# A hybrid decoder layer on one core: queries turned on VectorE ahead of their store instead of on TensorE after their load, and the norm vectors in one laid-out load

## The chip, the cores and the metric

The kernel runs on one core of a Trainium2 chip. The core has four engines that compute, each with its own instruction stream in program order: TensorE (PE: matrix products and transposes, which write to PSUM; its weight loads are shown apart as PEld), VectorE (DVE), ScalarE (ACT) and GpSimd (POOL). SyncE (SP) computes nothing and issues most of the DMAs; POOL and ACT issue a few. The metric is the device time of one execution in microseconds, as the median of several runs. The time before is 1201.64 us, the median of three (1200.92 to 1206.23).

## The reference

One layer (DEPTH 1) over x of 1024 tokens by 1024 channels, all in float32. A norm and one projection give queries, three pairs of keys and values, gates and the inputs of a short convolution. Attention runs over compressed, selected and windowed keys; its output and the convolution's go through an output projection, and a squared-ReLU MLP follows. Cut to what matters here:

```python
h = rms_norm(x, g_mix_norm[l])
z = h @ w_in[l]
q, kc, vc, ks_, vs_, kw_, vw_, gl, hc, cg, bg = jnp.split(z, offs, axis=-1)
q = rms_norm(q.reshape(B, T, N_ATTN_HEADS, HEAD_DIM), g_q[l])      # 8 heads of 64
k_cmp = rms_norm(compress(kc, pe, w1, b1, w2, b2), g_k[l, 0])
k_slc = rms_norm(ks_.reshape(kv_shape), g_k[l, 1])                 # 2 groups of 64
k_win = rms_norm(kw_.reshape(kv_shape), g_k[l, 2])
gates = jax.nn.sigmoid(gl)
attn_out = nsa_attention(q, k_cmp, v_cmp, k_slc, v_slc, k_win, v_win, gates)
conv_out = short_conv_mixer(hc, cg, bg, conv_w[l])
x = x + concat(rms_norm(attn_out, ...), rms_norm(conv_out, ...)) @ w_o[l]
h = rms_norm(x, g_ffn_norm[l])
x = x + jnp.square(jax.nn.relu(h @ w_up[l])) @ w_down[l]
```

Scores are products of a query with keys over the 64 channels of a head, so on TensorE both must stand with channels on the partitions.

## The kernel before

The 1024 tokens are eight blocks (tb) of 128. Numbers are split into a high part of reduced precision and the remainder, and a product is made of three matmuls (high by high, high by low, low by high) with 512 columns each; `copy_act` on ScalarE writes the high part, a subtraction on VectorE or POOL the low part.

**Order.** The code calls a planner (class `Plan`) in place of the engines. It records every instruction with what it depends on, gives each a modelled cost (`Plan.cost`), lays out the whole kernel in a model of the engines, and shakes the due times with the seeds in the tuple `SEEDS`, one after the other, to arrive at the order in which the instructions are then issued on each engine. `plan.follow` makes an instruction wait in that plan for others, and `plan.slack` lets the planner expect a DMA to land later than modelled by that many us. So an edit anywhere can move instructions everywhere. All recorded instructions bear the same line in the profile, L272, and are told apart by their tiles.

**Start.** The loads of x, of its transpose and of weights are issued on SP. `norm_in` (L751) loads an x block `xt`, sums its squares and keeps the load in the list `last`; `x_in` loads and splits parts of the transpose; `token_sums` adds and subtracts token halves (tiles x, t1, t2, t4) on VectorE, with high parts on ScalarE. At L786 to L790 the norm vectors g_q and g_k are loaded by POOL, each copied to all 128 partitions by the DMA, after the sixth `xt` load (`last[5]`) in the plan; VectorE then multiplies `gk_bc` by `gq_bc`. So g_q is applied to the keys, not to the queries. TensorE runs the first projection into PSUM tiles `zp` of a pool of five; ScalarE empties them to `z`, and `k_norm` (L834) scales the keys with `gk_bc`.

**Compression.** `compress_steps` (from L876) makes the compressed keys and values in small steps between the query blocks. Its biases `b1_bc` and `b2_bc`, for keys and values together, are loaded at L869 to L874 by POOL.

**Query projection.** For each of the eight blocks (loop at L964) ScalarE empties `zp` to `z`, the eight heads are normed, and `qn` is filled: per head 128 numbers, 64 of the high part and 64 of the low part, with the high part first for the heads of group 0 and second for those of group 1. The row of 1024 numbers of each token goes to the DRAM tile `q_d` in one DMA of 512 KB on SP. `qn` has one buffer.

**Attention.** `queries(tb)` (L1305) brings one block back. For each of two groups g it loads 256 KB of `q_d` into `qx` (one buffer), turns the four heads with one TensorE transpose each into a PSUM tile `tpq` of the pool `psP` (three buffers, tag pt, shared with the transposes of probabilities `tp`), and ScalarE copies `tpq` to `Qg` (three buffers). POOL then copies half of `Qg` to `Qz` (two buffers). `scores(tb, g, ...)` multiplies `Qg` and `Qz` with the keys; VectorE adds distances and takes the maxima (`nm`), ScalarE the exponentials (`pt`), POOL weighs them; `weigh` turns the probabilities (`tp`), splits them (`ph` on ScalarE, `pl` on VectorE) and multiplies with the values (`ot`); `finish` applies the output projection (`wa`). The blocks are taken in the order 3, 2, 1, 0, 4, 5, 7, 6; a block's queries are fetched while the block before it is worked on. The output projection of the convolution (`wc`) is mixed with the first block. The MLP follows, from about 570 us to the end.

Of the kernel before, what the change touches and what calls it, by code (L numbers as in the profile page):

```python
# [10 lines left out]
F32 = mybir.dt.float32  # L11
F32R = mybir.dt.float32r
# [136 lines left out]
        self.seen, self.nodes, self.tile = [], [], None  # L149


SEEDS = (1000006, 1000008, 1000012, 1000028, 1000030, 1000044, 1000056, 1000071, 1000072, 1000073, 1000097, 1000113, 1000123, 1000168, 1000170, 1000178, 1000184, 1000230, 1000235, 1000280, 1000295, 1000299, 1000300, 1000339, 1000349, 1000363, 1000373, 1000406, 1000407, 1000433, 1000445, 1000463, 1000475, 1000479, 1000518, 1000523, 1000551, 1000553, 1000556, 1000560, 1000561, 1000602, 1000631, 1000682, 1000684, 1000744, 1000762, 1000820, 1000883, 1000891, 1000903, 1000927, 1000943, 1000964, 1000972, 1001010, 1001014, 1001117, 1001141, 1001179, 1001212, 1001309, 1001376, 1001383, 1001417, 1001453, 1001528, 1001689, 1001701, 1001732, 1001749, 1001991, 1002049, 1002060, 1002190, 1002305, 1002330, 1002338, 1002354, 1002415, 1002550, 1002569, 1002695, 1002710, 1002984, 1002988, 1003029, 1003125, 1003214, 1003231, 1003262, 1003316, 1003351, 1003576, 1003644, 1003759, 1003795, 1004123, 1004570, 1004698, 1004784, 1004785, 1004924, 1005022, 1005212, 1005620, 1006475, 1006959, 1007873, 1008004, 1008352, 1008594, 1008648, 1008693, 1008873, 1008934, 1009028, 1009032, 1009107, 1009286, 1009381, 1009543, 1009791, 1009963, 1010063, 1010079, 1010468, 1010509, 1010514, 1010529, 1011124, 1011195, 1011915, 1011946, 1012041, 1012076, 1012380, 1012411, 1012893, 1013770, 1013959, 1014076, 1014304, 1014500, 1014729, 1014772, 1014939, 1015200, 1015293, 1016011, 1016217, 1016447, 1016524, 1016643, 1016685, 1017381, 1018464, 1019062, 1019171, 1019208, 1019743, 1019760, 1019965, 1020196, 1020244, 1020564, 1020709, 1022567, 1022787, 1023841, 1024288, 1025052, 1025417, 1026259, 1028122, 1028301, 1028583, 1029752, 1031086, 1031370, 1032572, 1032854, 1033263, 1033296, 1033397, 1033540, 1033583, 1033891, 1034930, 1036525,)


class Plan:
# [146 lines left out]
    def cost(self, name, method, a, kw, views):  # L302
# [23 lines left out]
        if name == "DVE":  # L326
            self.port = near and n > 1 and (method in ("tensor_tensor", "scalar_tensor_tensor", "tensor_copy")
                                            or method == "tensor_scalar" and n != 12)
            if method == "tensor_tensor_reduce":
                self.port = False  # L330
                c = .079 + n * .00104 + .06 * isinstance(kw.get("scalar"), View)
                return c, c + .13, 0
            if method == "scalar_tensor_tensor":
                c = .1 + n * .0011 if n >= 200 else .11 + n * .0012
            elif method == "tensor_scalar":
                c = .06 + n * .00059 + (.05 if n < 64 else 0)
            elif method == "memset":
# [262 lines left out]


@with_exitstack
def trunk_layer(ctx, tc, x, x_t, vectors, w_in, g_q, g_k, w_cmp1, b_cmp1, w_cmp2, b_cmp2,
                w_o, w_up, w_down, out):
# [4 lines left out]
    w_in, g_q, g_k = w_in[0], g_q[0], g_k[0]  # L609
# [12 lines left out]
    def tt(eng, o, a, b, op):  # L622
        eng.tensor_tensor(o, a, b, op=op)
# [63 lines left out]
    hTl = [(twp, htp)[i].tile([P, KD, 512], F32R, name=f"hTl{i}") for i in range(2)]  # L687

    kcn = twp.tile([P, 2 * HD], F32, name="kcn")
    gq_bc = twp.tile([P, HD], F32, name="gq_bc")  # L690
    gk_bc = twp.tile([P, 3, HD], F32, name="gk_bc")
    TD = {n: [htp.tile([P, 4, 512], F32R, name=f"{n}{q}") for q in "hl"] for n in ("t1", "t2")}
    wp = pool(wp_stack, "wp", bufs=4, side="right")
    psP_stack = ctx.enter_context(ExitStack())
# [88 lines left out]
        x_in(k, 1)  # L783
    for tb in range(4, NT):
        norm_in(tb)
    plan.follow = (last[5],)  # L786
    nc.gpsimd.dma_start(gq_bc, g_q.partition_broadcast(P))
    nc.gpsimd.dma_start(gk_bc, g_k.partition_broadcast(P))
    plan.follow = ()
    tt(nc.vector, gk_bc, gk_bc, gq_bc.unsqueeze(1).to_broadcast([P, 3, HD]), ALU.mult)  # L790

# [41 lines left out]
    with b1:  # L833
# [32 lines left out]
        xp_stack.close()  # L866
        cs = b1.enter_context(ExitStack())
        cp = pool(cs, "cp", side="right")
        b1_bc = cp.tile([P, 2, 256], F32, name="b1_bc")  # L869
        b2_bc = cp.tile([P, 2, HD], F32, name="b2_bc")  # L870
        plan.follow = (last[-1],)
        nc.gpsimd.dma_start(b1_bc, b_cmp1.partition_broadcast(P))
        nc.gpsimd.dma_start(b2_bc, b_cmp2.partition_broadcast(P))
        plan.follow = ()  # L874

        def compress_steps():  # L876
            for kv in range(2):
                yield
                ch = cp.tile([P, 16, HD], F32, name="ch")
                for g in range(G):  # L880
                    plan.slack = 3.5
# [39 lines left out]
                tt(nc.vector, hx, hp[:, :256], b1_bc[:, kv], ALU.add)  # L921
# [16 lines left out]
                if kv == 0:  # L938
# [4 lines left out]
                    tt(nc.vector, kc, cps[:, :HD], b2_bc[:, 0], ALU.add)  # L943
                    sq = cp.tile([P, HD], F32, name="kcsq")
                    ss = st.tile([P, 1], F32, name="ss")
                    nc.scalar.activation(sq, kc, AF.Square, accum_out=ss)
                    ri = st.tile([P, 1], F32, name="ri")
# [3 lines left out]
                else:  # L951
                    for g in range(G):
                        cps = psB.tile([P, 512], F32, name="cps", tag="mm")
                        for j in range(2):
                            nc.tensor.matmul(cps[:64, :HD], hT[:, j, g * 64:(g + 1) * 64], w2[:, j],
                                             start=j == 0, stop=j == 1)
                        vc = cp.tile([64, HD], F32, name="vcr")
                        tt(nc.vector, vc, cps[:64, :HD], b2_bc[:64, 1], ALU.add)
# [5 lines left out]
        for tb, ps in (a for tbs in (QUADS[1], (0,), (1,), (2,), (3,)) for a in z_tokens(pieces, tbs, 512, steps, 1)):  # L964
# [19 lines left out]

        plan.plus = 12
        for _ in steps:
# [22 lines left out]
    with ExitStack() as b2:  # L1009
# [809 lines left out]
    plan.issue()  # L1819


_INS = ['x', 'x_t', 'vectors', 'w_in', 'g_q', 'g_k', 'w_cmp1', 'b_cmp1', 'w_cmp2', 'b_cmp2', 'w_o', 'w_up', 'w_down']
# [32 lines left out]
```

## Time and profile before

| | us |
|---|---|
| median of three runs | 1201.64 |
| profiled execution | 1202.77 |
| its span, first to last instruction | 1201.0 |
| DVE busy in the span | 909.1 |
| ACT busy in the span | 698.4 |
| POOL busy in the span | 726.4 |

The profile shows one execution. A busy TensorE in it counts a matmul from its start to its modelled end; matmuls overlap, so what one costs the stream is read from the distance between starts. "A <- B" in brackets behind an instruction means that its engine stood idle before it and what released it. Times in the timeline are from the start of the span.

The transfers that the change deals with stand thus in the list of DMAs (KB each, and median us from issue to landing): q_d<-qn 8 of 512 KB, 4.2 us; qx<-q_d 16 of 256 KB, 2.7 us.

### The profile page before, as it was taken

The numbers are of one execution on the slowest core, as the hardware profiler recorded it, in microseconds if no ns is written. First come the engines' busy times: TensorE is split into PE (matmuls) and PEld (weight loads), VectorE is DVE, ScalarE is ACT, GpSimd is POOL, SyncE is SP. The second block draws the span as 40 slices with busy tenths as digits, with TensorE's granted clock in tenths as the row PEclk, the third lists the DMA queues.
The fourth block names the chain that finished last, engine by engine and source line by source line (L and its number), as shares of the span: only waits on it lengthen the run. The fifth ranks groups of instructions, "written<-read, shape, count | busy, mean of one in ns | idle before, by whom it ended". The sixth has DMA issues, their size and how long they took to land.

```text
span 1201.0 us, 18151 instructions
## 1 busy us (share of the span) xinstructions
PE 1189.2 (99%) x5893; PEld 991.4 (83%) x5893; DVE 909.1 (76%) x1800; ACT 698.4 (58%) x1551; POOL 726.4 (60%) x663
## 2 busy tenths in 40 slices
PE   9999999999999999999999999999999999999998
PEld 7788988888888888888788888888888888888887
DVE  7748868785798989998875665554468988888885
ACT  7678634352599878888855545555345434434440
POOL 1544400020376553534978878787889899888971
PEclk9999999999999999999999999999999999999999
DMA  9765531256112110003155354443559445543513
GB/s 337 184 166 180 167 79 36 71 175 211 46 52 71 36 36 19 27 19 109 50 167 176 121 186 141 149 158 132 184 192 399 145 149 177 168 163 112 163 44 140
DMA packets 106702, 160.24 MB, mean 133 GB/s; under 512 B 20592, under 2 KB 58752, under 8 KB 106608
## 3 DMA queue, kind: packets, MB, share of 16 engines
q1 hardware_dynamic: 100320, 151.25, 38.5%
q10 hardware_dynamic: 5520, 5.28, 1.3%
q0 software_dynamic: 768, 2.56, 0.8%
q8 instruction: 46, 0.75, 0.3%
q14 instruction: 48, 0.39, 0.1%
HBM read 110.82 MB, written 48.23 MB: 132 GB/s over the span
## 4 chain that ended last, share of the span: by engine, by line
PE 88%; DVE 5%; DMA 2%; ACT 2%; issue 1%; SPq 0%; POOL 0%; DVEq 0%; ACTq 0%
PE X L272 28%; PE Z L272 18%; PE tp L272 6%; PE zX L272 5%; PE zp L272 5%; PE ot L272 5%; PE wa L272 4%; PE wc L272 3%; PE W L272 3%; PE zZ L272 3%; PE zW L272 1%; PE hp L272 1%; DMA qx<-q_d 1%; DVE hTl L272 1%; DVE pl L272 1%
## 5 line engine op out<-in xcount | busy, mean ns | idle before, releaser
L272 PE MATMUL X<-we,uu 128*128 128x512 f32 x720 | 196.1, 389 | 0.1
L272 PE MATMUL Z<-we,uu 128*128 128x512 f32 (+1 forms) x582 | 163.5, 387 | 0.5 <-DVE y L272 0.5
L272 PEld LDWEIGHTS X<-we,uu 128*128 128x128 f32 x720 | 135.1, 188 | 28.6 <-DVE y L272 0.6
L272 ACT ACTIVATE uu<-ur 128x512 fp32r<-128x512 f32 x108 | 66.9, 631 | 131.6 <-PE Z L272 71.5
L272 PEld LDWEIGHTS Z<-we,uu 128*128 128x128 f32 x582 | 108.6, 188 | 23.0 <-DVE y L272 0.7
L272 ACT ACTIVATE pt<-pt,nm 128x640 f32<-128x640 f32 (+7 forms) x128 | 93.8, 735 | 26.8 <-DVE nm L272 26.5
L272 POOL TENSOR_TENSOR d<-d 128x512 f32<-128x512 f32 x64 | 98.7, 1558 | 10.0 <-DVE d L272 8.4
L272 DVE TENSOR_TENSOR pl<-tp,ph 128x512 fp32r<-128x512 f32 (+1 forms) x148 | 94.8, 654 | 6.5 <-ACT ph L272 5.3
L272 DVE TENSOR_TENSOR y<-X,y 128x512 f32<-128x512 f32 x128 | 84.2, 681 | 13.4 <-PE X L272 13.2
L272 PE MATMUL tp<-ident,pt 128*128 128x128 f32 x528 | 93.6, 273 | 0.4 <-DVE nm L272 0.4
L272 ACT ACTIVATE ph<-tp 128x512 fp32r<-128x512 f32 (+1 forms) x148 | 81.5, 571 | 17.5 <-PE tp L272 12.2
L272 DVE TENSOR_TENSOR y<-Z,y 128x512 f32<-128x512 f32 (+1 forms) x97 | 65.2, 681 | 31.6 <-PE Z L272 30.8
L272 POOL TENSOR_TENSOR uu<-ur,uu 128x512 fp32r<-128x512 f32 x54 | 83.4, 1547 | 3.2 <-ACT uu L272 3.1
L272 ACT ACTIVATE we<-s 128x512 fp32r<-128x512 f32 x55 | 34.6, 630 | 82.6 <-PE X L272 35.1
L272 PEld LDWEIGHTS tp<-ident,pt 128*128 128x128 f32 x528 | 67.2, 141 | 12.2 <-issue 0.8
L272 POOL MEMSET Qz<- 64x512 f32 x16 | 8.3, 520 | 111.1 <-PE zX L272 104.8
L272 PE MATMUL zp<-w_hi,hTh 128*128 128x512 f32 (+1 forms) x192 | 66.1, 369 | 3.2 <-ACT z L272 2.7
L272 PE MATMUL zp<-w_lo,hTh 128*128 128x512 f32 (+1 forms) x192 | 66.8, 364 | 0.0
L272 PE MATMUL zp<-w_hi,hTl 128*128 128x512 f32 (+1 forms) x192 | 65.4, 364 | 0.0
L272 POOL TENSOR_TENSOR we<-wd,we 128x512 fp32r<-128x512 f32 x32 | 46.9, 1467 | 29.1 <-ACT we L272 29.0
L272 POOL TENSOR_TENSOR pt<-pt,rr 128x640 f32<-128x640 f32 (+4 forms) x64 | 62.2, 1001 | 0.0
L272 ACT ACTIVATE we<-wu 128x512 fp32r<-128x512 f32 x57 | 35.9, 630 | 44.6 <-PE X L272 30.0
(1340 smaller groups left out, 3649.1 us busy)
## 6 DMA issues: line engine op xcount, KB each, us to landing
u_d<-d SPq DMA_DIRECT2D x112, 256.0 KB, 2.7
ur<-u_d SPq DMA_DIRECT2D x108, 256.0 KB, 2.9
wu<-in_w_up_dram SPq DMA_DIRECT2D x16, 1024.0 KB, 6.0
wd<-in_w_down_dram SPq DMA_DIRECT2D x16, 1024.0 KB, 6.9
xt<-in_x_dram SPq DMA_DIRECT2D x10, 512.0 KB, 7.1
x<-in_x_t_dram SPq DMA_DIRECT2D x16, 256.0 KB, 6.7
w1r<-in_w_cmp_dram SPq DMA_DIRECT2D x16, 256.0 KB, 2.8
q_d<-qn SPq DMA_DIRECT2D x8, 512.0 KB, 4.2
```

Source lines behind the costliest of these rows:

```text
L272: node.do.append(lambda: getattr(engine, method)(*[real(x) for x in a], **{k: real(x) for k, x in kw.items()}))
```

## The change

The queries are turned before they are stored. After `z` is scaled, VectorE transposes it in blocks of 32 by 32 into a new tile `zT` (one buffer): within each such block, channels stand on the partitions and tokens along the row. ScalarE and VectorE write the high and low parts of `zT` to `qn`, whose row is now ordered by group, by quarter c (two of the high part and two of the low part, each 32 channels), by head and by 32 tokens. The store to `q_d` keeps its size and its one DMA.

`queries` loads each group in four DMAs of 64 KB on SP, one for each quarter: it puts the four 32-partition blocks of a quarter side by side in 32 partitions of `qx`. So `qx` holds 128 channels on the partitions, and ScalarE copies it to `Qg` with its dimensions swapped. The transposes on TensorE and the PSUM tile `tpq` are gone.

The norm vectors come from the host as one array `g_qk` of 128 rows (the same 256 numbers on each) and are loaded by SP in one DMA, after the second `xt` load in the plan, with a slack of 3 us. The biases of the compression are loaded for keys and values apart, the second pair into the same buffer. Squares of the compressed keys go to a tile that exists already. The planner gets a price for VectorE's transpose, and a new tuple of seeds (203 in place of 190).

```diff
+            if method == "transpose":
+                self.port = True
+                return .07 + n * .00104, .15 + n * .00104, 0
...
-    gq_bc = twp.tile([P, HD], F32, name="gq_bc")
-    gk_bc = twp.tile([P, 3, HD], F32, name="gk_bc")
+    g_bc = twp.tile([P, 4, HD], F32, name="g_bc")
+    gq_bc, gk_bc = g_bc[:, 0], g_bc[:, 1:]
...
-    plan.follow = (last[5],)
-    nc.gpsimd.dma_start(gq_bc, g_q.partition_broadcast(P))
-    nc.gpsimd.dma_start(gk_bc, g_k.partition_broadcast(P))
+    plan.follow = (last[1],)
+    plan.slack = 3.0
+    nc.sync.dma_start(g_bc, g_qk.rearrange("p (n d) -> p n d", d=HD))
+    plan.slack = 0.0
     plan.follow = ()
     tt(nc.vector, gk_bc, gk_bc, gq_bc.unsqueeze(1).to_broadcast([P, 3, HD]), ALU.mult)
...
-        b1_bc = cp.tile([P, 2, 256], F32, name="b1_bc")
-        b2_bc = cp.tile([P, 2, HD], F32, name="b2_bc")
-        plan.follow = (last[-1],)
-        nc.gpsimd.dma_start(b1_bc, b_cmp1.partition_broadcast(P))
-        nc.gpsimd.dma_start(b2_bc, b_cmp2.partition_broadcast(P))
-        plan.follow = ()
...
             for kv in range(2):
                 yield
+                b1_bc = cp.tile([P, 256], F32, name="b1_bc")
+                b2_bc = cp.tile([P, HD], F32, name="b2_bc")
+                plan.follow = () if kv else (last[-1],)
+                nc.gpsimd.dma_start(b1_bc, b_cmp1[kv].partition_broadcast(P))
+                nc.gpsimd.dma_start(b2_bc, b_cmp2[kv].partition_broadcast(P))
+                plan.follow = ()
...
-                    sq = cp.tile([P, HD], F32, name="kcsq")
+                    sq = zt.tile([P, HD], BF16, name="ksq", bufs=2)
...
-            qn = zt.tile([P, H, 2, HD], F32R, name="qn", bufs=1)
+            qn = zt.tile([P, G, 4, R, 32], F32R, name="qn", bufs=1)
             zh = z.rearrange("p (h d) -> p h d", h=H)
             tt(nc.vector, zh, zh, ri.unsqueeze(2).to_broadcast([P, H, HD]), ALU.mult)
+            zT = zt.tile([P, 512], F32, name="zT", bufs=1)
+            nc.vector.transpose(zT, z)
             for g in range(G):
-                zg = z[:, g * 256:(g + 1) * 256].rearrange("p (r d) -> p r d", r=R)
-                qg = qn[:, g * R:(g + 1) * R]
-                copy_act(qg[:, :, g], zg)
-                tt(nc.vector, qg[:, :, 1 - g], zg, qg[:, :, g].bitcast(F32), ALU.subtract)
-            nc.sync.dma_start(q_d[tb * P:(tb + 1) * P], qn.rearrange("p h a d -> p (h a d)").bitcast(F32))
+                zg = zT[:, g * 256:(g + 1) * 256].rearrange("p (r c t) -> p c r t", r=R, c=2)
+                hi, lo = qn[:, g, 2 * g:2 * g + 2], qn[:, g, 2 - 2 * g:4 - 2 * g]
+                copy_act(hi, zg)
+                tt(nc.vector, lo, zg, hi.bitcast(F32), ALU.subtract)
+            nc.sync.dma_start(q_d[tb * P:(tb + 1) * P], qn.rearrange("p g c r t -> p (g c r t)").bitcast(F32))
...
-                qx = kp.tile([P, R, 2, HD], F32, name="qx", bufs=1)
-                q_load.append(nc.sync.dma_start(qx.rearrange("p h a d -> p (h a d)"),
-                                                q_d[tb * P:(tb + 1) * P, g * 512:(g + 1) * 512]))
-                tp = psP.tile([P, 4, P], F32, name="tpq", tag="pt")
-                for r in range(R):
-                    nc.tensor.transpose(tp[:, r], qx[:, r].rearrange("p a d -> p (a d)"), ident)
+                qx = kp.tile([P, 4, R, 32], F32, name="qx", bufs=1)
+                for c in range(4):
+                    q_load.append(nc.sync.dma_start(
+                        qx[c * 32:(c + 1) * 32].rearrange("p b r t -> p b (r t)"),
+                        q_d[tb * P:(tb + 1) * P, (4 * g + c) * P:(4 * g + c + 1) * P].rearrange("(b p) n -> p b n", b=4)))
                 Qg = kp.tile([P, R, P], F32R, name="Qg", bufs=3)
                 Qz = kp.tile([P, R, P], F32R, name="Qz", bufs=2)
-                copy_act(Qg, tp)
+                copy_act(Qg.rearrange("p r (b t) -> p b r t", b=4), qx)
...
+    a["g_qk"] = np.tile(np.concatenate([a[n].reshape(-1) for n in ("g_q", "g_k")]), (P, 1))
```

More of the change, by code (lines that the diff above doesn't have):

```diff
@@ L149, in __init__ @@
         self.seen, self.nodes, self.tile = [], [], None
-SEEDS = (1000006, 1000008, 1000012, 1000028, 1000030, 1000044, 1000056, 1000071, 1000072, 1000073, 1000097, 1000113, 1000123, 1000168, 1000170, 1000178, 1000184, 1000230, 1000235, 1000280, 1000295, 1000299, 1000300, 1000339, 1000349, 1000363, 1000373, 1000406, 1000407, 1000433, 1000445, 1000463, 1000475, 1000479, 1000518, 1000523, 1000551, 1000553, 1000556, 1000560, 1000561, 1000602, 1000631, 1000682, 1000684, 1000744, 1000762, 1000820, 1000883, 1000891, 1000903, 1000927, 1000943, 1000964, 1000972, 1001010, 1001014, 1001117, 1001141, 1001179, 1001212, 1001309, 1001376, 1001383, 1001417, 1001453, 1001528, 1001689, 1001701, 1001732, 1001749, 1001991, 1002049, 1002060, 1002190, 1002305, 1002330, 1002338, 1002354, 1002415, 1002550, 1002569, 1002695, 1002710, 1002984, 1002988, 1003029, 1003125, 1003214, 1003231, 1003262, 1003316, 1003351, 1003576, 1003644, 1003759, 1003795, 1004123, 1004570, 1004698, 1004784, 1004785, 1004924, 1005022, 1005212, 1005620, 1006475, 1006959, 1007873, 1008004, 1008352, 1008594, 1008648, 1008693, 1008873, 1008934, 1009028, 1009032, 1009107, 1009286, 1009381, 1009543, 1009791, 1009963, 1010063, 1010079, 1010468, 1010509, 1010514, 1010529, 1011124, 1011195, 1011915, 1011946, 1012041, 1012076, 1012380, 1012411, 1012893, 1013770, 1013959, 1014076, 1014304, 1014500, 1014729, 1014772, 1014939, 1015200, 1015293, 1016011, 1016217, 1016447, 1016524, 1016643, 1016685, 1017381, 1018464, 1019062, 1019171, 1019208, 1019743, 1019760, 1019965, 1020196, 1020244, 1020564, 1020709, 1022567, 1022787, 1023841, 1024288, 1025052, 1025417, 1026259, 1028122, 1028301, 1028583, 1029752, 1031086, 1031370, 1032572, 1032854, 1033263, 1033296, 1033397, 1033540, 1033583, 1033891, 1034930, 1036525,)
@@ new lines @@
+SEEDS = (2000001, 2000009, 2000013, 2000017, 2000022, 2000032, 2000044, 2000058, 2000081, 2000085, 2000102, 2000104, 2000108, 2000117, 2000118, 2000120, 2000124, 2000145, 2000184, 2000186, 2000196, 2000208, 2000238, 2000239, 2000245, 2000249, 2000260, 2000265, 2000288, 2000371, 2000377, 2000382, 2000411, 2000418, 2000436, 2000441, 2000461, 2000474, 2000495, 2000500, 2000527, 2000574, 2000576, 2000635, 2000720, 2000761, 2000774, 2000782, 2000842, 2000883, 2000911, 2000936, 2000967, 2000969, 2000973, 2000988, 2000991, 2001020, 2001029, 2001098, 2001100, 2001110, 2001120, 2001144, 2001190, 2001202, 2001248, 2001320, 2001349, 2001433, 2001445, 2001448, 2001471, 2001476, 2001508, 2001568, 2001633, 2001780, 2001785, 2001802, 2001917, 2001946, 2001999, 2002101, 2002182, 2002190, 2002242, 2002280, 2002412, 2002457, 2002551, 2002612, 2002635, 2002688, 2002703, 2002749, 2002860, 2002866, 2002987, 2003017, 2003047, 2003055, 2003093, 2003147, 2003222, 2003490, 2003533, 2003849, 2003884, 2003930, 2003960, 2004590, 2004906, 2004971, 2004977, 2005120, 2005164, 2005329, 2005350, 2005450, 2005837, 2005910, 2006173, 2006416, 2007354, 2007479, 2007505, 2008545, 2009341, 2009523, 2009532, 2009747, 2009808, 2010018, 2010533, 2010770, 2011774, 2011993, 2012221, 2012263, 2012540, 2012574, 2012638, 2012822, 2012884, 2012941, 2013085, 2013281, 2013381, 2013387, 2013409, 2013428, 2013552, 2013705, 2013779, 2013847, 2014081, 2014918, 2015206, 2015428, 2015848, 2016209, 2016481, 2016763, 2016817, 2017424, 2017730, 2018518, 2018824, 2019350, 2019403, 2020765, 2021342, 2021690, 2022635, 2022874, 2023049, 2025027, 2025556, 2025662, 2026004, 2026715, 2027431, 2027556, 2029434, 2030520, 2030934, 2033024, 2033371, 2033439, 2034388, 2035227, 2038505, 2039056, 2039889, 2042865, 2043237, 2045309, 2046744, 2046873, 2047128, 2050898, 2056562,)
@@ L602, in trunk_layer @@
 @with_exitstack
-def trunk_layer(ctx, tc, x, x_t, vectors, w_in, g_q, g_k, w_cmp1, b_cmp1, w_cmp2, b_cmp2,
+def trunk_layer(ctx, tc, x, x_t, vectors, w_in, g_qk, w_cmp1, b_cmp1, w_cmp2, b_cmp2,
                 w_o, w_up, w_down, out):
@@ L608, in trunk_layer @@
     out2d = out.rearrange("b t d -> (b t) d")
-    w_in, g_q, g_k = w_in[0], g_q[0], g_k[0]
+    w_in = w_in[0]
     w_cmp1, b_cmp1, w_cmp2, b_cmp2 = w_cmp1[0], b_cmp1[0], w_cmp2[0], b_cmp2[0]
@@ L920, in compress_steps @@
                 hx = cp.tile([P, 256], F32, name="hx")
-                tt(nc.vector, hx, hp[:, :256], b1_bc[:, kv], ALU.add)
+                tt(nc.vector, hx, hp[:, :256], b1_bc, ALU.add)
                 th = cp.tile([P, 256], F32, name="th", tag="th")
@@ L942, in compress_steps @@
                     kc = cp.tile([P, HD], F32, name="kc")
-                    tt(nc.vector, kc, cps[:, :HD], b2_bc[:, 0], ALU.add)
-                    sq = cp.tile([P, HD], F32, name="kcsq")
+                    tt(nc.vector, kc, cps[:, :HD], b2_bc, ALU.add)
+                    sq = zt.tile([P, HD], BF16, name="ksq", bufs=2)
                     ss = st.tile([P, 1], F32, name="ss")
@@ L957, in compress_steps @@
                         vc = cp.tile([64, HD], F32, name="vcr")
-                        tt(nc.vector, vc, cps[:64, :HD], b2_bc[:64, 1], ALU.add)
+                        tt(nc.vector, vc, cps[:64, :HD], b2_bc[:64], ALU.add)
                         copy_act(VC[0][:64, g, 0:HD], vc)
@@ L1819, in trunk_layer @@
     plan.issue()
-_INS = ['x', 'x_t', 'vectors', 'w_in', 'g_q', 'g_k', 'w_cmp1', 'b_cmp1', 'w_cmp2', 'b_cmp2', 'w_o', 'w_up', 'w_down']
+_INS = ['x', 'x_t', 'vectors', 'w_in', 'g_qk', 'w_cmp1', 'b_cmp1', 'w_cmp2', 'b_cmp2', 'w_o', 'w_up', 'w_down']
 _OUTS = [((1, T, D), 'float32')]
```

## The prediction

> **What bounds the kernel now.** The page's shares come first, then busy time by stage, then the chain of work that ended last.
>
> ```profile
> PE 1189.2 (99%) x5893; PEld 991.4 (83%) x5893; DVE 909.1 (76%) x1800; ACT 698.4 (58%) x1551; POOL 726.4 (60%) x663
> ```
>
> ```profile
> PE 88%; DVE 5%; DMA 2%; ACT 2%; issue 1%; SPq 0%; POOL 0%; DVEq 0%; ACTq 0%
> ```
>
> TensorE is busy nearly all the time and owns 88% of the chain, so what an edit does to TensorE's own stream decides. In the next table the columns are length, then busy us (and instructions) of PE, PEld, DVE, ACT and POOL, granted clock, DMA share, GB/s.
>
> ```profile
> 0.00:25.00 25.00, 23.41 (x100) 19.75 (x101) 18.27 (x33) 19.02 (x29) 3.82 (x17) 1.00 0.95 343
> 25.00:42.00 17.00, 14.31 (x62) 11.35 (x61) 13.76 (x31) 11.99 (x30) 6.85 (x9) 0.98 0.73 217
> ...
> 75.00:127.00 52.00, 51.57 (x320) 45.34 (x318) 40.16 (x90) 41.76 (x160) 24.98 (x19) 1.00 0.51 161
> ...
> 282.00:490.00 208.00, 205.85 (x1238) 175.42 (x1236) 178.25 (x638) 162.11 (x400) 103.86 (x174) 1.00 0.17 58
> ```
>
> The change touches three stages: the start (25 to 42 us), the query projection (75 to 127), and attention while queries are still being loaded (282 to 490). Only the first has a TensorE hole worth naming, 17.00 - 14.31 = 2.7 us. After 490 nothing is edited.
>
> **The norm vectors.** The order of instructions around the hole:
>
> ```profile
> 39.51 0.36 DVE L272 TENSOR_TENSOR gk_bc<-gk_bc,gq_bc 128x192 f32<-128x192 f32 x1 [3.17 <-DMA gk_bc<-in_g_k_dram]
> 39.78 0.69 DVE L272 TENSOR_TENSOR x<-x,x 128x512 f32<-128x512 f32 x1
> ...
> 40.51 0.63 ACT L272 ACTIVATE t4h<-x 128x512 fp32r<-128x512 f32 x1 [3.20 <-DVE x L272]
> ...
> 41.04 0.67 ACT L272 ACTIVATE z<-zp,rmix 128x512 f32<-128x512 f32 x1
> ```
>
> VectorE ends its work at 39.51 - 3.17 = 36.34 and stands at the product gk_bc*gq_bc until the load that POOL issued has landed. Behind it in its order is a token sum x, behind that on ScalarE t4h, and behind t4h the copy z that empties TensorE's PSUM bank. TensorE:
>
> ```profile
> 38.68 0.40 PE L272 MATMUL zp<-w_lo,hTh 128*128 128x512 f32 x1
> 41.76 0.79 PE L272 MATMUL zp<-w_hi,hTh 128*128 128x512 f32 x1 [2.69 <-ACT z L272]
> ...
> 44.90 0.39 PE L272 MATMUL zp<-w_lo,hTh 128*128 128x512 f32 x1
> 45.13 0.40 PE L272 MATMUL zp<-w_hi,hTl 128*128 128x512 f32 x1
> ```
>
> From 45.13 - 44.90 one matmul takes 0.23 us of the stream. From 38.68 to 41.76 are 3.08 us for one matmul: 2.85 us lost. Then seven matmuls take 44.90 - 41.76 = 3.14 us where 7 x 0.23 = 1.61 would do, because the clock drops behind the hole:
>
> ```profile
> 42.00:45.40 3.40, 3.40 (x10) 2.65 (x11) 2.80 (x8) 3.04 (x10) 3.40 (x4) 0.58 0.47 95
> ```
>
> That is 1.53 us more, 4.4 us in all. The new load is placed on SP behind the second xt load instead of on POOL behind the sixth; these are issued at 9.5 and 28.2 us:
>
> ```profile
> 9.46 0.33 SPq L272 DMA_DIRECT2D xt<-in_x_dram  x1
> ```
>
> ```profile
> 28.18 0.33 SPq L272 DMA_DIRECT2D xt<-in_x_dram  x1
> ```
>
> So it comes some 19 us earlier, and the wait goes with 10 us and more to spare. What is late next: without the stall, product (0.36), x (0.69), t4h (0.63) and z (0.67) from 36.34 end near 38.7, and TensorE has matmuls until 38.68 + 0.23 = 38.9. The hole closes, just. I take -4.4; the bounds are 0, if another wait stands there, and -4.4. The cost: 128 KB more in a queue that moves 343 GB/s, 0.4 us for whoever waits for a later x or weight load; I take +0.2 (0 to +0.4). POOL loses two DMA issues and later gains two for the split biases, whose loads land many us ahead of use: 0.
>
> **The turned queries.** Removed from TensorE are 8 x 2 x 4 = 64 transposes. Their stated duration is pipelined; the stream's share is read from neighbouring starts:
>
> ```profile
> 282.63 0.40 PE L272 MATMUL wc<-hTh,MCh 128*128 128x512 f32 x1
> 282.87 0.38 PE L272 MATMUL tpq<-ident,qx 128*128 128x128 f32 x2
> ...
> 283.00 0.48 PE L272 MATMUL wc<-hTl,MCh 128*128 128x512 f32 x1
> ```
>
> Two of them take 283.00 - 282.63 - 0.23 = 0.14 us, 0.07 each. On the chain, three take 0.33, 0.11 each:
>
> ```profile
> 288.63 0.33 PE tpq L272 x3
> ```
>
> So 64 are 4.5 to 7.0 us. Not all of it comes back: in 282 to 490 VectorE is busy 178.25 of 208 us (86%), and where it is late TensorE's slots are free anyway. The chain there is TensorE's in the main, with shares as follows:
>
> ```profile
> by line: PE ot L272 17.5%; PE tp L272 14.2%; PE wa L272 13.3%; PE wc L272 11.2%; DMA qx<-q_d 3.9%; DVE pl L272 3.1%; DVE pt L272 3.1%; PE tpq L272 2.9%; issue 2.1%; ACT pt L272 1.7%; ACT ph L272 1.5%; ACT jk L272 1.0%; DVE w_lo L272 1.0%; P
> ```
>
> 2.9% of 208 us are 6.0 us of tpq on it. I take 60%, -3.6 us (bounds -0.5 and -7.0).
>
> ScalarE's copy to Qg reads SBUF instead of PSUM:
>
> ```profile
> L272 ACT ACTIVATE Qg<-tpq x16: 588/597/601, 283.7 to 489.3; 128x512 fp32r<-128x512 f32 x16
> ```
>
> ```profile
> L272 ACT ACTIVATE w1h<-w1r 128x512 fp32r<-128x512 f32 x14 | 8.7, 622 | 2.6 <-DMA w1r<-in_w_cmp_dram 2.3
> ```
>
> 16 x 25 ns are 0.4 us on an engine busy 162 of 208: nothing. The permuted output keeps runs of 32 numbers; no row shows what that costs, and I take the contiguous price.
>
> The loads: 16 of 256 KB become 64 of 64 KB, all on SP. The first row is TensorE's idle time before qx (us, times); then the nearest rows for the new loads, which end with us from issue to landing:
>
> ```profile
>   DMA qx<-q_d: 1.7, 4
> ```
>
> ```profile
> 40.89 1.26 SPq L272 DMA_DIRECT2D k_d<-krow  x2
> ```
>
> ```profile
> qx<-q_d SPq DMA_DIRECT2D x16, 256.0 KB, 2.7
> ...
> k_d<-krow SPq DMA_DIRECT2D x32, 64.0 KB, 2.5
> ```
>
> By k_d a 64 KB DMA holds SP 0.63 us and lands in 2.5; the fourth lands 3 x 0.63 + 2.5 = 4.4 us after the first issue, 1.7 later than now. The wait moves too: now TensorE waits for qx (1.7 us in 4 waits), then ScalarE's Qg copy will, with ph splits and exponentials of other blocks queued behind it. qx has one buffer, released by that copy instead of by the transposes, 0.6 us later. Cover is ample mostly; this load is used 37 us on:
>
> ```profile
> 403.69 0.32 SPq L272 DMA_DIRECT2D qx<-q_d  x1
> ```
>
> ```profile
> 440.99 0.60 ACT L272 ACTIVATE Qg<-tpq 128x512 fp32r<-128x512 f32 x1 [0.66 <-PE tpq L272]
> ```
>
> SP issues little else here (DMA share 0.17). I take +0.3 (0 to +2: eight second heads, 1.7 late, hidden but for a seventh part).
>
> [...]
>
> VectorE gets 8 transposes of 128x512 f32 between 75 and 127 us. No row shows one; the nearest are a cheap and a dear form of that size in one pass:
>
> ```profile
> L272 DVE TENSOR_SCALAR x<-x,cols 128x512 f32<-128x512 f32 x16 | 7.5, 502 | 0.2
> ...
> L272 DVE TENSOR_TENSOR we<-wu,we 128x512 fp32r<-128x512 f32 x38 | 46.4, 1231 | 19.3 <-PE X L272 10.1 <-ACT we L272 8.5 <-PE W L272 0.6
> ```
>
> I take 0.6 us, nearer the first, since a transpose too has one operand, both ends in SBUF; 4.8 in all: VectorE goes from 40.2 to 45 of 52 us. TensorE's lead (51.57 of 52 busy) covers most; behind a transpose stand w1l and hT, which TensorE does wait for. +0.8 (0 to +3, the latter at 1.23 us each, 50 of 52).
>
> **Sum.** -4.4 + 0.2 - 3.6 + 0.3 + 0.8 = -6.7 us. The profiled execution took 1202.77 us (span 1201.0, 1.8 around it), so it would take 1196.1. The runs shown have their median 1.1 lower, at 1201.64; from there 1194.9, said as 1195. The order of all instructions is planned anew, so small waits move everywhere; the range carries that.
>
> **Rivals.** *VectorE paces attention* (0.20): freed slots stay empty, since the next tp waits for DVE nm or pl. For it: 86% busy, and DVE pl and pt on the chain; against it: tpq itself on the chain with 2.9%. The removal brings 0.5, and the time is 1201.6 - 4.4 + 0.2 - 0.5 + 0.3 + 0.8 = 1198. [...]
>
> *The hole is not closed* (0.12): the margin of 0.2 us above is thin, and VectorE has no other idle from 25 to 36 us. If ScalarE's z is late by another wait, 4.4 us stay: 1199.3.
>
> *Attention runs freer* (0.12): all 7.0 us come back, with 1.7 us of TensorE's qx waits, and 16 PSUM tiles of the pool that tp shares are free: 1201.6 - 4.4 - 8.7 + 1.3 = 1190.
>
> *The transposes bind the projection* (0.06, the slower side): VectorE has 52 - 40.2 = 11.8 us to give to 8 of them, so above 1.5 us each it becomes the stage's bound. At 3 us each (four passes) it adds 24 - 11.8 = 12.2: 1201.6 - 7.5 + 12.2 = 1206. Against it: no form of this size in the rows needs over 1.23 us.
>
> **Chances and range.** The forecast has 0.50, within 1190.5 and 1199. About 0.5%, 6 us, is what a measurement of this kernel can tell from no change, so faster means below 1195.6: three fifths of the forecast, all of the freer case, a sixth of the first rivals, 0.47. Slower means above 1207.7, the dear transposes or a bad new order, 0.06. The rest, 0.47, lies between. The range from 1188 to 1202 reaches over both ends of the tpq term and the open hole, and leaves out the dear transposes.
>
> **What would show it.** Right: no TensorE idle above 1 us between 25 and 45 us and a clock of 1.00 there; gk_bc loaded before 25 us; VectorE transposes near 0.6 us and 45 us of VectorE in the projection; no tpq; Qg copies near 0.62 us with little wait for DMA; attention's end some 3 to 4 us nearer to the projection's end. Wrong: a new hole with a dropped clock, ScalarE waiting for qx by more than 2 us in all, transposes above 1.2 us, or attention as long as before.

## The result and the profile after

The changed kernel took 1193.8 us, the median of four runs (1192.05 to 1194.33), beside 1201.78 us for the kernel before, also four runs (1200.92 to 1206.23). The ratio is 0.9924 [0.9897, 0.995]: 8.0 us less, where the forecast was 6.7 us less and 1195.0 us. The profiled execution took 1192.05 us with a span of 1190.3 us, 10.7 us shorter than the profiled execution before; it is the fastest of the four, so the rows below show more than the medians.

The page of the changed kernel, busy times and the chain that ended last, each answering to the line shown of before:

```profile
PE 1180.9 (99%) x5829; PEld 982.5 (83%) x5829; DVE 912.8 (77%) x1808; ACT 696.7 (59%) x1551; POOL 721.0 (61%) x663
...
PE 91%; DVE 4%; ACT 2%; DMA 1%; issue 1%; POOL 1%; SPq 0%; ACTq 0%; DVEq 0%; POOLq 0%
```

TensorE has 5893 - 5829 = 64 matmuls less, the 64 transposes. It is still busy 99% of the span, and its share of the chain rose from 88% to 91%: what else was on the chain shrank more than TensorE did.

The same stretches as before, from the table by stage of the changed kernel (length, then busy us and instructions of PE, PEld, DVE, ACT and POOL, granted clock, DMA share, GB/s):

```profile
25.00:42.00 17.00, 17.00 (x75) 13.84 (x74) 16.56 (x37) 14.46 (x37) 8.80 (x11) 1.00 0.80 232
75.00:127.00 52.00, 51.89 (x329) 46.24 (x328) 45.14 (x99) 39.84 (x165) 25.89 (x22) 1.00 0.55 172
282.00:490.00 208.00, 205.38 (x1216) 173.26 (x1215) 182.91 (x656) 168.80 (x414) 106.79 (x178) 1.00 0.15 48
```

Between 25 and 42 us TensorE has no idle time left (14.31 busy before, 17.00 now) and does 75 matmuls instead of 62. In the projection VectorE went from 40.16 to 45.14 us, and TensorE is as full as it was. In attention the engines are not less busy; in the same 208 us they are further on (VectorE 656 instructions instead of 638).

Where the stages end tells where the time went. These rows give, for three groups of matmuls, the start of the first and the last one; zp is the projections of the start and of the queries, wc the products behind the compression, wa the last ones that belong to attention. Before, then after:

```profile
L272 PE MATMUL zp<-w_hi,hTl x192: 285/390/628, 8.1 to 144.9; 128*128 128x512 f32 x128, 128*128 128x280 f32 x64
...
L272 PE MATMUL wc<-hTh,MCl x64: 387/390/478, 256.8 to 314.3; 128*128 128x512 f32 x64
...
L272 PE MATMUL wa<-w_lo,mh x64: 387/393/485, 353.8 to 585.5; 128*128 128x512 f32 x64
```

```profile
L272 PE MATMUL zp<-w_hi,hTl x192: 287/390/486, 6.7 to 139.0; 128*128 128x512 f32 x128, 128*128 128x280 f32 x64
...
L272 PE MATMUL wc<-hTh,MCl x64: 387/393/478, 252.2 to 307.1; 128*128 128x512 f32 x64
...
L272 PE MATMUL wa<-w_lo,mh x64: 387/393/485, 344.8 to 573.6; 128*128 128x512 f32 x64
```

From the start to the last zp the changed kernel needs 144.9 - 139.0 = 5.9 us less; from there to the last wc 168.1 instead of 169.4; from there to the last wa 266.5 instead of 271.2, 4.7 less; and from there to the end 616.7 instead of 615.5. The split at wc is not a clean one, since the first queries are turned before the last wc; from the last zp to the last wa, which holds all 64 of the removed transposes, it is 434.6 instead of 440.6, 6.0 less. So the gain lies in two places, the start and attention, as the sum had it. Of the start's 5.9 us, 1.4 are there at the first of these matmuls already (6.7 and 8.1). That part differs from one execution to the next: in the changed kernel run again (below) the first stands at 7.6 and the last zp at 139.6, 5.3 us earlier than before.

### The profile page after: what moved, and what is told of

The parts are those of the page before. It is cut to its first block, busy times and chain, and to the rows that moved or that the text cites. A ratio compares the mean times of both kernels' runs of the same rounds, so it can differ in the third digit from the quotient of the medians.

```text
span 1190.3 us, 18120 instructions
## 1 busy us (share of the span) xinstructions
PE 1180.9 (99%) x5829; PEld 982.5 (83%) x5829; DVE 912.8 (77%) x1808; ACT 696.7 (59%) x1551; POOL 721.0 (61%) x663
## 4 chain that ended last, share of the span: by engine, by line
PE 91%; DVE 4%; ACT 2%; DMA 1%; issue 1%; POOL 1%; SPq 0%; ACTq 0%; DVEq 0%; POOLq 0%
PE X L272 28%; PE Z L272 17%; PE zp L272 9%; PE tp L272 6%; PE zX L272 5%; PE ot L272 5%; PE wa L272 4%; PE wc L272 4%; PE W L272 3%; PE zZ L272 3%; PE zW L272 1%; PE hp L272 1%; DMA u_d<-d 1%; DVE y L272 1%; DVE pl L272 1%
## 5 line engine op out<-in xcount | busy, mean ns | idle before, releaser
L272 PE MATMUL tp<-ident,pt 128*128 128x128 f32 x528 | 96.0, 273 | 1.6 <-DVE pl L272 1.3
L272 DVE TENSOR_TENSOR we<-wu,we 128x512 fp32r<-128x512 f32 x38 | 48.4, 1281 | 20.0 <-PE X L272 11.2
```

What stands on the lines that cost most here:

```text
L272: node.do.append(lambda: getattr(engine, method)(*[real(x) for x in a], **{k: real(x) for k, x in kw.items()}))
```

## The experiments

Three theories stood against each other. *The forecast's:* the norm vectors give back the hole at 39 us, and the removed transposes give back TensorE time in attention. *VectorE paces attention:* the removed transposes are worth next to nothing, and the gain is the start's. *The order:* all instructions are planned anew with new seeds, and the gain is a luckier order. The runs stand in three groups, and each ratio is to the kernel before on the same chip. Differences between kernels are taken from the ratios, with 1202 us for 1; by the intervals such a difference is good to 2 or 2.5 us either way.

### The changed kernel again

The changed kernel beside the first group, to be compared with.

> The changed kernel itself, beside the others of this call. By the medians shown, 8 us below the kernel before (ratio 0.9924, 0.9897 to 0.995); by the two profiled executions 10.7 us. I expect 8 to 9 us, ratio 0.9925 to 0.9935, and use it as the base of the next two runs.

Measured: 1193.79 us beside 1202.11, ratio 0.9932 [0.9918, 0.9945], 8.2 us less. The numbers below are set against this run.

### TensorE's transposes put back, as dummy work

The order of the changed kernel; after each copy to Qg, four transposes of the identity go into the next group of tp, whose own transposes then overwrite them.

```diff
+            due = 0
             for n in order:
+                if due and n in self.firsts:
+                    due -= 1
+                    for r in range(4):
+                        self.tc.nc.tensor.transpose(n.out.tile[:, r % 4], self.ident.real(), self.ident.real())
                 for f in n.do:
                     f()
+                due += n in self.extra
...
```

> The changed kernel, its order kept, with 64 transposes of 128x128 given back to TensorE in attention, four ahead of each of 16 groups of tp transposes, into the same PSUM tile; they wait for nothing of their own and nobody reads them. Theory (TensorE's stream paces attention): 3.6 us more, at most 7.0. Rival (VectorE paces attention, freed slots stay empty): 0 to 1 us more. TensorE's slots alone, by the rows of the kernel before, are 4.5 to 7.0 us.

Measured: 1198.55 us, ratio 0.9971 [0.9961, 0.9981], so 0.0039 or 4.7 us more than the changed kernel. The rows of wc and wa for the changed kernel again, then for this one:

```profile
L272 PE MATMUL wc<-hTh,MCl x64: 387/393/478, 252.8 to 307.7; 128*128 128x512 f32 x64
...
L272 PE MATMUL wa<-w_lo,mh x64: 387/393/483, 346.8 to 575.6; 128*128 128x512 f32 x64
```

```profile
L272 PE MATMUL wc<-hTh,MCl x64: 387/393/478, 252.8 to 307.7; 128*128 128x512 f32 x64
...
L272 PE MATMUL wa<-w_lo,mh x64: 387/393/483, 347.6 to 580.1; 128*128 128x512 f32 x64
```

The two stand at the same 307.7 us and are 4.5 us apart at the end of attention. That is 64 times 0.07 us, the price read from neighbouring starts. VectorE would have hidden this if it were the pace. Work added to the changed kernel is not quite work taken from the kernel before; the pair of kernels without seeds, below, is a second witness for that.

### Twice as many

The same with eight transposes instead of four at each place, 128 in all: if VectorE had some slack left for TensorE, the second 64 would cost more than the first; if none of it was hidden, about the same.

> The changed kernel, its order kept, with 128 transposes given to TensorE in attention, eight in each of the 16 places where the run with 64 had four. With 64 it was 4.8 us slower, 0.074 us each, the low end of what the rows give. If TensorE's stream is the bound throughout, the second 64 cost 0.109 us each, the pure slot, 7.0: 11 to 12 us more than the changed kernel. If waits on VectorE swallow a part, at most as much again: 9 to 10 us.

Measured: 1206.26 us beside 1203.79, ratio 1.0024 [1.0015, 1.0034]: 0.0053 or 6.4 us more than with 64, 11.1 more than with none. The row of wa, then the stretch of attention from the table by stage:

```profile
L272 PE MATMUL wa<-w_lo,mh x64: 387/394/483, 350.1 to 586.9; 128*128 128x512 f32 x64
```

```profile
350.00:586.00 236.00, 235.42 (x1462) 202.19 (x1461) 205.65 (x690) 198.51 (x459) 125.48 (x190) 1.00 0.13 45
```

The same stretch of the changed kernel run again, cut at its own times:

```profile
346.00:575.00 229.00, 228.41 (x1388) 194.12 (x1387) 205.78 (x691) 198.92 (x463) 126.47 (x192) 1.00 0.14 46
```

VectorE does the same work in both (205.65 and 205.78 us, 690 and 691 instructions) and merely has 7 us more for it; TensorE is busy all but 0.6 us in both. So TensorE's stream sets the length of attention, although VectorE is busy 90% of it (205.78 of 229). The first 64 cost 0.07 each and the second 0.10, but this difference lies within the intervals; all 128 cost 11.1 us, 0.087 each.

### The norm vectors late again

The order of the changed kernel, with the one load of g_bc moved to just ahead of the product that needs it.

```diff
+        moved, at = self.late          # the load of g_bc; the product gk_bc*gq_bc
+        order.remove(moved)
+        order.insert(order.index(at), moved)
...
```

> The changed kernel, its order kept, with the one load of the norm vectors moved back on SP's queue to right ahead of the product that needs it. Theory: VectorE stands 4 to 6 us at the product, TensorE's hole of 2 to 5 us comes back with a clock near 0.5 behind it, 3.5 to 6 us more than the changed kernel. Rival (the new order has enough work ahead on TensorE to cover it): under 1 us more.

Measured: 1195.37 us, ratio 0.9945 [0.9931, 0.996], 1.6 us more than the changed kernel, with overlapping intervals, where 3.5 to 6 were expected. The start and the stretch behind the hole in the table by stage, and the product in the timeline:

```profile
25.00:42.00 17.00, 14.93 (x59) 11.77 (x58) 14.40 (x33) 12.09 (x32) 6.44 (x8) 0.91 0.72 210
...
39.10:42.40 3.30, 3.30 (x9) 2.59 (x8) 3.30 (x9) 2.42 (x9) 1.66 (x3) 0.50 0.54 116
```

```profile
35.91 0.36 DVE L272 TENSOR_TENSOR g_bc<-g_bc 128x192 f32<-128x192 f32 x1 [2.33 <-DMA g_bc<-in_g_qk_dram]
```

The late load alone brings back all that the kernel before showed, if in smaller size: VectorE's wait (2.33 us), 2.1 us of idle TensorE, and the clock at 0.50 behind it. In this profiled execution the last zp starts at 142.8 us, 3.2 later than in the changed kernel again (139.6). At the end 2.4 us of that are left by the two spans (1194.2 and 1191.8), 1.6 by the ratios.

### The norm vectors early, in the kernel before

The kernel before with its own order, and only its two norm loads moved: issued by SP ahead of the fifth xt load.

```diff
...
+        to = self.norms
+        for n, (o, i) in zip(moved, to):
+            n.do = [lambda o=o, i=i: self.tc.nc.sync.dma_start(o.real(), i.partition_broadcast(P))]
...
+        order = [n for n in order if n not in moved]
+        i = order.index(at)            # last[4]
+        order[i:i] = moved
...
```

> The kernel before, its order kept, with the two loads of the norm vectors alone taken from POOL's queue to SP's, ahead of the fifth xt load, where the changed kernel has its one load (21.8 us). The run with the early loads on POOL lost as much ahead of 20 us as it won at 39, since POOL, waiting for nothing, issued them at 1.9 us among the first loads of x and weights. Theory (the late load makes the hole, and a place behind the first loads costs nothing): no hole at 39 us, none above 1.2 us at 8 us, clock 1.00 from 8 to 300 us, 4.4 us less than before: 1197.7, and at least 3. Rival (the projection is short of something else, which the hole only hid): under 1.5 us less.

Measured: 1198.38 us, ratio 0.9969 [0.9956, 0.9982], 3.7 us less than before. Three stretches of its table by stage:

```profile
25.00:42.00 17.00, 17.00 (x75) 13.86 (x74) 16.32 (x38) 15.16 (x40) 9.44 (x10) 1.00 0.76 241
42.00:45.40 3.40, 3.40 (x17) 2.75 (x16) 3.40 (x10) 3.40 (x10) 2.69 (x4) 1.00 0.37 89
60.00:64.00 4.00, 3.98 (x17) 3.09 (x18) 2.90 (x5) 2.28 (x7) 1.94 (x2) 1.00 0.85 217
```

In the order of before, the hole at 39 us closes completely and the clock stays at 1.00, so the chain from the product over x and t4h to z was read rightly. But then something else is late, in the timeline:

```profile
57.05 0.63 ACT L272 ACTIVATE w1h<-w1r 128x512 fp32r<-128x512 f32 x1 [3.43 <-DMA w1r<-in_w_cmp_dram]
...
58.93 1.04 ACT L272 ACTIVATE w_hi<-w_raw 128x1024 fp32r<-128x1024 f32 x1
...
60.02 0.73 PE L272 MATMUL zp<-w_hi,hTh 128*128 128x512 f32 x2 [1.96 <-ACT w_hi L272]
```

ScalarE stands at w1h until a weight load of the compression has landed, behind it stands w_hi, and TensorE waits 1.96 us for that. Before, TensorE's wait at this place was 0.30 us. Of the 4.4 us that the hole and its clock cost, about 1.7 were given back here. The order of the changed kernel doesn't have this wait.

### The norm vectors early by the wrong queue

The kernel before, with the two loads left on POOL and moved in the order to behind the second xt load.

```diff
...
+        order = [n for n in order if n not in moved]
+        i = order.index(at) + 1        # last[1]
+        order[i:i] = moved
...
```

> The kernel before, its order kept on every engine, with the two loads of the norm vectors alone moved ahead on POOL's queue, behind the second xt load in the plan. Theory (the hole and the dropped clock come from this load): no TensorE idle above 0.5 us between 25 and 45 us, clock 1.00 there, and 4.4 us less in all, of which 2.85 for the hole and 1.53 for the clock: 1197.4. Rival 1 (something else is late at the same place, so the hole stays): 0 us. Rival 2 (the hole goes, but the time is lost again before attention ends): TensorE's projection ends 4.4 us earlier and the whole kernel less than 1 us.

Measured: 1203.42 us, ratio 1.0006 [0.9997, 1.0015], no gain where 4.4 us were expected. The timeline and a stretch:

```profile
1.88 0.73 POOL L272 DMA_DIRECT2D gq_bc<-in_g_q_dram  x1
...
12.95 1.65 PE L272 MATMUL zp<-w_hi,hTh 128*128 128x512 f32 x3 [4.34 <-ACT hTh L272]
```

```profile
12.10:18.90 6.80, 5.95 (x14) 4.69 (x15) 6.58 (x11) 6.05 (x11) 0.00 (x0) 0.50 1.03 397
38.00:42.00 4.00, 4.00 (x19) 3.24 (x18) 4.00 (x10) 4.00 (x11) 1.98 (x2) 1.00 0.77 213
```

The hole at 39 is gone, and a larger one stands at 8 us with 6.8 us of clock at 0.50 behind it. The place in the planned order did not hold the two loads back: POOL's last memset ahead of them starts at 1.63 us, and it issued them at 1.88 and 2.61 us, among the first loads of x and weights. Over the first 13 us the DMA engines are about as busy in both kernels (share 0.86 before, 0.84 here) but move 221 GB/s here instead of 295; ScalarE then waits 4.66 us for a weight load, and TensorE 4.34 us for ScalarE. This miss is why the run above uses SP.

### The hole filled with work

The kernel before with 20 dummy transposes on TensorE where the hole stands, to keep its clock up and thus to price the clock's part.

```diff
+            seen = 0
             for n in order:
+                seen += n.engine == "PE"
+                if n.engine == "PE" and seen == 161:
+                    for _ in range(20):
+                        self.tc.nc.tensor.transpose(self.warm.real()[:, :P], self.ident.real(), self.ident.real())
...
```

> The kernel before, its order kept, with 20 transposes of the identity given to TensorE where its hole at 39 us lies, ahead of the matmul that waits there; nobody reads them. VectorE still waits for the load, and the hole's matmul still starts when z is copied. Theory (the clock drop behind the hole costs 1.53 us of its own): clock 1.00 there, TensorE's next seven matmuls in 1.6 us instead of 3.1, and 1.5 us less than before. Rival (the slow matmuls have another cause): no difference, or the 20 transposes end late and cost up to 1 us.

Measured: 1203.91 us, ratio 1.0015 [1.0003, 1.0027], 1.8 us more than before. The timeline and the stretches behind the hole and around 61 us:

```profile
41.73 0.50 PE L272 MATMUL zp<-w_hi,hTh 128*128 128x512 f32 x1 [0.46 <-ACT z L272]
...
43.45 0.39 PE L272 MATMUL zp<-w_lo,hTh 128*128 128x512 f32 x1
```

```profile
42.00:45.40 3.40, 3.40 (x16) 2.73 (x16) 2.80 (x8) 3.40 (x11) 3.40 (x3) 1.00 0.48 96
60.50:63.50 3.00, 1.00 (x5) 0.51 (x4) 1.67 (x5) 2.84 (x9) 1.17 (x2) 1.00 0.89 229
63.70:67.00 3.30, 3.30 (x9) 2.63 (x8) 2.42 (x3) 1.91 (x7) 1.75 (x2) 0.50 0.81 194
```

The seven matmuls that took 3.14 us at the low clock take 43.45 - 41.73 = 1.72 us here, so the clock's part was 1.4 us (1.53 in the sum). The kernel still became slower: TensorE came 1.4 us earlier to the place at 61 us, waited there 2.0 us for the same w_hi instead of 0.30, and the clock fell there instead. The 1.5 us less that were expected did not come. This is a second sighting of what is late next.

### VectorE's transposes twice

The changed kernel with each transpose of z issued two times.

```diff
-                for f in n.do:
+                for f in n.do * (2 if n in self.extra else 1):
                     f()
...
```

> The changed kernel, its order kept, with each of VectorE's 8 transposes of the queries done twice. They measure 0.70 us each in the changed kernel, so VectorE gets 5.6 us more between 70 and 121 us. My account (+0.8 for 8 of them): 0.8 to 1.5 us more. Rival 1 (TensorE's lead covers them all): under 0.3. Rival 2 (VectorE is at its limit there): 3 us or more.

Measured: 1194.84 us, ratio 0.9939 [0.9923, 0.9955], 0.8 us more than the changed kernel, which is within the intervals. The last zp starts at 141.6 us instead of 139.6. In the changed kernel one transpose takes 0.70 us (the row of the tile zT: minimum, median and maximum in ns, first and last start):

```profile
L272 DVE STREAM_TRANSPOSE zT<-z x8: 698/701/711, 69.4 to 120.1; 128x512 f32<-128x512 f32 x8
```

So 5.6 us of VectorE cost 0.8 us, and by the intervals at most about 3: partly or wholly covered, and no new bound. This prices eight more transposes, not the eight that the change brought.

### The loads twice

The changed kernel with each of the 64 loads of qx issued two times.

> The changed kernel, its order kept, with each of the 64 loads of queries issued twice on SP, the second time with the same data into the same place. My account (+0.3 for 48 more issues and 1.7 us later landing): 0.3 to 0.6 us more. Rival (SP or the DMA engines are short there, or ScalarE's Qg copies come late): 2 us or more, seen as ScalarE waiting for qx.

Measured: 1250.23 us, ratio 1.039 [1.0375, 1.0405]. The waits of ScalarE and of SP's queue, each us, times, longest:

```profile
ACT Qg L272 <- DMA qx<-q_d: 58.6, 8, 13.9
```

```profile
SPq L272 <- DMA qx<-q_d: 144.5, 79, 6.3
```

This was not the test it was meant to be. SP waited 79 times for a load of qx to land, 144.5 us in all (19 times and 24.1 us in the changed kernel): the second load to a place stood until the first had landed, so the loads came one after the other, and what was queued on SP behind them stood too. It says nothing on the price of 48 more issues. With 8 waits of 58.6 us on ScalarE the kernel loses 55 us, so late queries can decide; how much of the 55 is theirs alone is not shown.

### The order

Three kernels with other seeds: the kernel before with the seeds of the changed kernel, and each of the two with no seeds at all, that is, in the planner's first order.

```diff
-SEEDS = (1000006, 1000008, ...)
+SEEDS = ()
```

> The kernel before with nothing changed but the planner's seeds, which are those of the changed kernel: another order of the same work. It sizes what a new order alone is worth. If the order matters little: within 2 us of before. If the order found for the other kernel is bad for this one: 3 to 8 us slower.

> The kernel before with no seeds at all: the planner's first order, not shaken. The run with the other kernel's seeds was 29 us slower, so an order that was not sought for the kernel costs much. Expected 10 to 30 us slower than before. It is the base for the next run: the same change with neither order sought.

> The changed kernel with no seeds: its first order, not shaken. If the gain lies in the edits themselves (TensorE's slots and the early norm load), this one is 5 to 10 us below the unshaken kernel before, in the norm vectors' stage and in attention. If it lies in the order that was sought anew, the two unshaken kernels are within 3 us of each other.

Measured: the kernel before with the other seeds 1231.03 us, ratio 1.0236 [1.0216, 1.0255]; without seeds the kernel before 1207.35 us, 1.0036 [1.0023, 1.0049], and the changed kernel 1201.02 us, 0.9982 [0.9973, 0.9991]. Seeds chosen for one kernel cost the other 28 us, where at most 8 were expected, so they can't be compared across kernels; the kernel before without seeds is 4.3 us slower, where 10 to 30 were expected. Without any, the changed kernel is 0.0054 or 6.5 us ahead. Most of the 8.2 us is thus there without the shaken order. The rest, 1.7 us, may come from a search that went better for the changed kernel; the intervals are wider than that.

Where the unshaken pair differs, before and then changed:

```profile
L272 PE MATMUL wa<-w_lo,mh x64: 387/393/480, 355.6 to 588.1; 128*128 128x512 f32 x64
```

```profile
L272 PE MATMUL wa<-w_lo,mh x64: 387/393/482, 350.6 to 581.8; 128*128 128x512 f32 x64
```

The last zp starts at 141.7 and 139.9 us. So from the last zp to the last wa the changed kernel needs 441.9 us instead of 446.4, 4.5 less: the transposes' part, in another pair of orders. At the start it wins only 1.8; in this order of before TensorE waits just once for z to empty a zp, 1.1 us, where the shaken order had 2.7, and the mean clock of the profiled execution is 1.000.

## Why the prediction was right, point by point

The bound was right: TensorE's own stream. The sum's sign, both of its large terms and their places came out, and the time is 1.2 us below the forecast. That it lies so near is in part luck: the start's term was too large and the transposes' too small, and the two partly cancel.

**The norm vectors, -4.4 + 0.2.** The mechanism is shown, with a smaller size that depends on the order: in the order of before, moving the loads alone gives 3.7 us (0.9969 [0.9956, 0.9982]); in that of the changed kernel, the load put back late costs 1.6, which is not clear of the noise. The hole and the clock drop behind it are there in both shaken orders with the load late, and gone in both with it early. What the step left out is the second late load, w1r at 58 us: it asked what is late next only up to 39 us. The argument of the thin margin (z at 38.7, TensorE out of work at 38.9) held in the order of before. In the changed kernel it was not needed, since there the product comes at 33.49 us:

```profile
21.76 0.46 SPq L272 DMA_DIRECT2D g_bc<-in_g_qk_dram  x1
...
33.49 0.35 DVE L272 TENSOR_TENSOR g_bc<-g_bc 128x192 f32<-128x192 f32 x1
```

One sign was named wrongly: the load was to be there before 25 us, 19 us earlier than now. It is issued at 21.76 and lands 6.4 us later, at 28.2. The second xt load was only the earliest place for it in the plan.

**The removed transposes, -3.6.** The mechanism was right and the size too small: 64 of them cost 4.7 us when put back, as dummy work in the same order (by the intervals 3.6 is not excluded by this run alone), 128 cost 11.1, and the unshaken pair gives 4.5. The step that was off is the share, 60% of what the chain showed. The price per transpose, 0.07 to 0.11, was right (0.087 over the 128), and nearly all 64 counted. VectorE's 86% had been allowed to hide too much. In attention (282 to 490 us) the profile before already had TensorE busy 205.85 of 208 us, and its waits for VectorE there came to 1.4 us; that was the better witness (us, times, longest):

```profile
PE ot L272 <- DVE pl L272: 1.0, 3, 0.5
...
PE tp L272 <- DVE nm L272: 0.4, 1, 0.4
```

The sign named for this term, attention's end 3 to 4 us nearer to the projection's, was passed: 6.0 us nearer in the first profiled execution and 4.6 in the changed kernel again (139.6 to 575.6).

**ScalarE's copy, 0, and the loads, +0.3.** The rows of the tile qx in the changed kernel, SP's holding time of one load, the copy, and ScalarE's idle time before it:

```profile
L272 SPq DMA_DIRECT2D qx<-q_d x64: 302/432/2778, 250.8 to 454.7; - x64
L272 ACT ACTIVATE Qg<-qx x16: 617/632/664, 261.8 to 476.0; 128x512 fp32r<-128x512 f32 x16
...
  DMA qx<-q_d: 3.7, 1
...
DMA to landing us min/median/max: 1.9/2.2/8.8
```

The copy takes 0.63 us (0.62 taken), and a 64 KB load holds SP 0.43 us and lands in 2.2 (0.63 and 2.5 taken). ScalarE waits 3.7 us, over the 2 us that were named as a sign against the forecast. It is one wait, before the first copy, at 258 to 261.8 us, where SP had issued two loads of y, and two of kn, between the four of qx:

```profile
250.79 0.81 SPq L272 DMA_DIRECT2D qx<-q_d  x2
251.64 2.14 SPq L272 DMA_DIRECT2D y<-in_x_dram  x2
...
254.31 0.50 SPq L272 DMA_DIRECT2D qx<-q_d  x1
...
255.33 0.51 SPq L272 DMA_DIRECT2D qx<-q_d  x1
```

TensorE works on wc there, and its waits from 250 to 275 us come to 0.2 us, for something else. So the sign was badly set: TensorE had no wait that answers to ScalarE's 3.7 us. The cost of the loads by themselves was not measured.

**VectorE's transposes, +0.8.** 0.70 us each where 0.6 was taken, 45.14 us of VectorE in the projection where 45 was; doubling them costs 0.8 us, give or take more than that. What the eight themselves cost was not measured.

**The sum.** Measured one by one the parts give -3.7 - 4.7 + 0.8 = -7.6 us with the norm loads in the order of before, and -1.6 - 4.7 + 0.8 = -5.5 with the load in that of the changed kernel, beside -8.2 for the whole; the 0.8 is that of eight more transposes. The rest, 0.6 to 2.7 us, is about the size of the intervals, and what is left to the order, to TensorE's former waits for qx and to the split biases stays open.

**The rivals.** *VectorE paces attention* fell with the two runs of dummy transposes: 64 of them on TensorE lengthened the stage by 4.5 us and 128 by 11.4 (from the last wc at 307.6 to the last wa at 586.9, beside 267.9). *The hole is not closed* was not so here, but its kin was: in the order of before a wait of 2 us opened at 58 us. *Attention runs freer* came half true: nearly all of the transposes' time came back, and the waits of tpq for qx went, but with 4.6 to 6.0 us from the last zp to the last wa, not 8.7. *The transposes bind the projection* did not come: 0.70 us is far below the 1.5 us from which they would.

No experiment beat the changed kernel.

## What to carry to other kernels

When two engines are both near their limit, an average share doesn't say which one paces; here the waits of one for the other did (1.4 us in 208), and a few dummy instructions on one of them, in two amounts (64 cost 4.7 us, 128 cost 11.1), tested it directly. When a stall goes, follow the order past the place where it stood to the next load that is only just in time, since part of the gain may be paid there (a wait of 1.96 us at 60 us here). And look at what the engine that issues a load has ahead of it in the written order: on POOL, which was done with that, the load was issued at 1.88 us here, among the loads that the start waits for.

## What was not expected of the hardware

The clock drop does not follow from the length of a wait alone. In the two profiled executions of the changed kernel TensorE has the same pause, 1.5 us from start to start with 1.16 us idle. The timelines of the first and of the second, and the stretches behind the pause:

```profile
323.93 0.34 PE L272 MATMUL s__3674<-KL,Qz 128*128 128x384 f32 x1
325.42 0.63 PE L272 MATMUL tp<-ident,pt 128*128 128x128 f32 x4 [1.16 <-DVE pl L272]
```

```profile
328.00:331.40 3.40, 3.40 (x23) 2.81 (x23) 3.40 (x10) 3.30 (x9) 1.00 (x3) 1.00 0.28 78
```

```profile
324.52 0.34 PE L272 MATMUL s__3674<-KL,Qz 128*128 128x384 f32 x1
326.02 0.63 PE L272 MATMUL tp<-ident,pt 128*128 128x128 f32 x4 [1.16 <-DVE pl L272]
```

```profile
328.20:331.50 3.30, 3.17 (x11) 2.60 (x12) 2.96 (x9) 2.52 (x6) 0.78 (x2) 0.50 0.37 84
```

In the first the clock stays at 1.00, in the second it is at 0.50 from 328.2 to 331.5 us (1.00 from 324 to 328 and from 332 to 336), and about half of the matmuls get done there (11 against 23). Idle times of 1.96 us (norm loads on SP, up to 60.0 us) and 2.0 us (hole filled, at 61 us) also differ: behind the first the clock is 1.00 from 60 to 64 us, behind the second 0.50 from 63.7 to 67.0. The drops that were read last 3.4 us in the kernel before (41 to 45 us at a mean of 0.57, so 3.4 at 0.50), at least 3.3 in the changed kernel again, with the norm load late (39.1 to 42.4) and with the hole filled, and 6.8 behind the wait of 4.34 with the early loads on POOL (12.1 to 18.9). What sets their length, and what besides the wait decides whether the clock falls, no run here shows. Drops stand behind 1.16 us (with two shorter waits after it, 0.34 and 0.32), 2.0, 2.1 and 2.69 us of idle time. So a pause of TensorE can cost more than its length: 1.4 us more behind the 2.69 (3.14 against 1.72 us for the seven matmuls above), and behind the 1.16 the clock fell in one execution and not in the other.
